# One more pair of expert-weight slots where v and the compressed rows were, and compressed columns copied unscaled in a written order of three engines

## The chip, the cores and the metric

The kernel runs on one core of one Trainium2 chip. The metric is the device time of one execution in microseconds. Everything is fp32; T = 256 tokens, D = 1024.

## What is computed

Two transformer blocks. The first is attention in two kinds, a gate, and a mixture of experts; the second a mixer, a feed-forward part and a gated projection. Cut to what matters here:

```
h = rms_norm(x, attn_norm_w)
c_q, c_kv, k_rope, dq, dk, dv, g_mla, g_diff = split(h @ w_in)        # 256, 256, 32, 5 x 1024 columns
q  = rms_norm(c_q,  mla_q_norm_w)  @ mla_w_uq                         # 16 heads x 96
kv = rms_norm(c_kv, mla_kv_norm_w) @ mla_w_ukv                        # 16 heads x (64 k + 64 v)
o_mla  = softmax attention of normed, rotated q and k
o_diff = difference of two softmax attentions with a distance bias
x = x + (sigmoid(g_mla) * o_mla + sigmoid(g_diff) * o_diff) @ w_out
h2 = rms_norm(x, ffn_norm_w)
affinity = softmax(h2 @ router_w); each of 16 experts takes its 32 best tokens
y_e = (silu(h2_e @ w_gate_e) * (h2_e @ w_up_e)) @ w_down_e            # three matrices of 8 MB per expert
x = x + the sum of the experts' rows
then a second block on x: rms_norm @ w_in, mixer, w_out, w_ff1, w_ff2, gated projection
```

## The kernel before, in words

**Stages.** The front (0 to 262 us) does the first block up to w_out. The router follows (to 277 us), then the 16 experts (to about 1165 us), then the second block. One expert's weights are 12 loads of 2 MB: four of `expert_w_gate`, four of `expert_w_up`, four of `expert_w_down`; all 192 together are some 400 MB.

**The front.** Products are made of three matmuls each (`mm3`, lines 209 to 211) of rounded parts: a weight piece is cast by ScalarE into `wh` (line 120), VectorE subtracts that from the weight into `wl` (line 121), and the pieces wait in three pairs of buffers (`split`, `put`, `take`; `AHEAD` says how many pieces are prepared ahead). `mla` begins with the transposes of x, eight `step`s over w_in's first 544 columns into four banks, the copies of these columns into `cc` (scaled by `rx`, the inverse root mean square of x: line 203 on ScalarE, line 205 on VectorE), the transposes of `cc` into the compressed rows `ch`, and then `up`: groups of six matmuls of 128x512 that go through three PSUM banks, first six groups for q (`put_q`, evicted by line 654 on ScalarE and VectorE in turn), then eight for k and v (`put_kv`, scaled by `rc`, the inverse root mean squares of the compressed rows). `rsqrt` (lines 90 to 98) is a chain of twelve small VectorE instructions. Sums of squares of q are taken by ScalarE (line 674) and reduced by VectorE (line 675). `tables` makes the tables of the rotation on GpSimd and ScalarE.

**What sets the order.** TensorE and GpSimd run in the order of the program. ScalarE and VectorE are ordered by a scheduler, except inside `manual_schedule` blocks, where they too run as written. Loads of weights are issued by SyncE's queue, in order: an issue that waits for its buffer holds up those behind it.

**The slots of the expert weights.** A ring of slots of 2 MB each is opened when the front closes. `SLOTS` names the slots of the first eleven loads: numbers from 0 are `ring2` pools (`R2` = 6 of them), -1 are two `ring1` pools, and -2 are places used once, which borrow buffers of the front (`once`: pairs of 1 MB halves loaded by line 299, or one whole). A load into a `ring2` or `ring1` slot goes through line 294, and the slot goes to the ring's end. So from load 11 on the slots come round in the order of `SLOTS` without the -2: eight slots. Load 11, the last of expert 0, takes the slot of load 0; load 12 that of load 2. In expert 0 the matmuls of the gate (line 1213) stand in turn with those that gather the tokens' rows (line 1170). The last expert closes three `ring2` slots for the second block's weight pieces; the second block's weights use the rest of the ring and `ring3` pools.

Of the kernel before, what the change touches and what calls it, by code (L numbers as in the profile page):

```python
# [23 lines left out]
R1, R2 = 4, 6  # L24
# [3 lines left out]
SLOTS = (3, -2, 2, 1, -2, 0, -1, -1, 4, 5, -2)  # L28
WSPLIT = 1088
AHEAD = 2  # L30
# [44 lines left out]
class Kernel:  # L75
# [233 lines left out]
    def run(self):  # L309
        self.cms, self.wide = {}, set()  # L310
        self.cp = self.open("cp")
        self.sm = self.open("sm", 2)
        r1 = self.ring = [self.open("ring1", side="right") for _ in range(R1)]
# [5 lines left out]
        with self.psum(mm=2, s=2, su=1, tr=2, o=1):  # L319
# [8 lines left out]
            ppool = self.open("pp", side="right")  # L328
# [16 lines left out]
            self.ring.append(self.open("ring3", side="right"))  # L345
# [5 lines left out]
            self.ring += [self.open("ring3", side="right") for _ in range(3)]  # L351
# [5 lines left out]
    def once(self):  # L357
# [7 lines left out]

        yield first
# [82 lines left out]
    def tables(self):  # L449
# [3 lines left out]
        nc.sync.dma_start(pos_c, A["positions"].rearrange("o (t p) -> p (o t)", p=128))  # L453
        pos_r = fp.tile([128, T], I32, name="pos_r")
        nc.sync.dma_start(pos_r, A["positions"].to_broadcast((128, T)))
# [20 lines left out]
        g.tensor_scalar(ang, ang, PI_IN, -PI_IN, op0=ALU.min, op1=ALU.max)  # L476
        di = fp.tile([128, NT, T], I32, name="di", tag="d1")
# [12 lines left out]
        self.lr = fp.tile([128, 4, 64], F32, name="lr")  # L490
# [11 lines left out]
    def lam(self):  # L502
# [18 lines left out]
        lp = fp.tile([128, 2, 64], F32, name="lp")  # L521
# [34 lines left out]
    def front(self):  # L556
# [19 lines left out]
        self.fp = fb = Parts(fs, (fd, same("d0", "d1")), (fv, same("v", "dist", "tab", "pos_r", "lr")),  # L576
                             (fe, same("d2")))
# [6 lines left out]
    def mla(self, fb):  # L584
        nc, A, g, ap = self.nc, self.A, self.nc.gpsimd, self.ap
        xh, xl = self.xh, self.xl
# [10 lines left out]
        with self.tc.manual_schedule(engines={mybir.EngineType.Activation, mybir.EngineType.DVE}):  # L597
            next(self.const)
            put(range(4))
            pss = [[self.bank("s"), self.bank("mm")] for t in range(NT)]  # L600
            self.ahead = 0
            self.look()
            put(range(4, 8))
            self.ahead = 1
            ws = []
            tables = self.tables()
            for k in range(8):
                ws = ws or self.take()
                step(k, *ws.pop(0))
                if k == 2:  # L610
                    next(tables)
                if k == 6:
                    next(tables)
                if k == 4:
                    self.rx = rx = self.rms(self.fa, self.x, self.od)
            cc = fb.tile([128, NT, 544], F32, name="cc", tag="d0")
# [9 lines left out]
        self.transpose_split(cc, self.col["mla_q_norm_w"], h, l, range(4), ("tr", "o", "tr", "mm"))
        sc = self.sm.tile([128, 2, NT], F32, name="sc", tag="sc")
        for i in range(2):
            self.sumsq(sc[:, i, :], cc[:, :, 256 * i : 256 * i + 256], cn[:, :, 256 * i : 256 * i + 256])
        rc = fb.tile([128, 2, NT], F32, name="rc")  # L630
        self.rsqrt(rc, sc, 1.0 / 256)

        qk = self.qp.tile([128, 2, NT, 16, 96], F32, name="qk", tag="qk")
# [566 lines left out]
    def experts(self, rp, r2, ppool, late):  # L1200
# [110 lines left out]
        for r in reversed(r2[:3]):  # L1311
            self.close(r)
# [457 lines left out]
```

## Time and profile of the kernel before

| what | us |
|---|---|
| median of three runs | 1506.15 (1505.64 to 1506.5) |
| profiled execution, its own time | 1505.89 |
| its span in the trace | 1504.2 |
| TensorE busy | 1138.1 (76%) |
| VectorE busy | 475.5 (32%) |
| ScalarE busy | 354.8 (24%) |
| DMA, mean of the span | 327 GB/s (427 in the experts) |

The page cuts the span into 40 slices of 37.6 us. TensorE is nearly always busy in slices 1 to 7 (front and router) and in the last ten (second block); in between, the DMA engines are.

### The profile page before, as it was taken

The numbers are of one execution on the slowest core, as the hardware profiler recorded it, in microseconds if no ns is written. First come the engines' busy times: TensorE is split into PE (matmuls) and PEld (weight loads), VectorE is DVE, ScalarE is ACT, GpSimd is POOL, SyncE is SP. The second block draws the span as 40 slices with busy tenths as digits, with TensorE's granted clock in tenths as the row PEclk, the third lists the DMA queues.
The fourth block names the chain that finished last, engine by engine and source line by source line (L and its number), as shares of the span: only waits on it lengthen the run. The fifth ranks groups of instructions, "written<-read, shape, count | busy, mean of one in ns | idle before, by whom it ended". The sixth has DMA issues, their size and how long they took to land.

```text
span 1504.2 us, 16611 instructions
## 1 busy us (share of the span) xinstructions
PE 1138.1 (76%) x6821; PEld 627.1 (42%) x6821; DVE 475.5 (32%) x969; ACT 354.8 (24%) x644; POOL 133.0 (9%) x181
## 2 busy tenths in 40 slices
PE   7999999885655566556565555656556899999998
PEld 6777897431111121111111111111111597889986
DVE  6987787410000000000000000000000477655456
ACT  5565655100000010000000000000000455554444
POOL 4613111000000000000000000000000134011010
PEclk9999999998688787887877888787877999999999
DMA  7533339999999999999999999999999972655520
GB/s 250 184 109 103 111 117 357 426 426 427 427 427 427 424 427 428 427 427 429 426 427 427 427 427 427 427 427 427 427 427 418 360 262 92 216 173 192 198 110 29
DMA packets 74842, 492.61 MB, mean 327 GB/s; under 512 B 5593, under 2 KB 10014, under 8 KB 50446
## 3 DMA queue, kind: packets, MB, share of 16 engines
q1 hardware_dynamic: 74366, 490.69, 80.7%
q8 instruction: 53, 0.87, 0.2%
q0 software_dynamic: 400, 0.86, 0.2%
q14 instruction: 23, 0.19, 0.0%
HBM read 490.48 MB, written 1.05 MB: 327 GB/s over the span
## 4 chain that ended last, share of the span: by engine, by line
DMA 50%; PE 37%; DVE 6%; issue 2%; ACT 1%; SPq 1%; POOL 1%; ACTq 0%; DVEq 0%
DMA w<-in_expert_w_down_dram 17%; DMA w<-in_expert_w_gate_dram 17%; DMA w<-in_expert_w_up_dram 15%; PE tr L1213 5%; PE mm L209 5%; PE mm L210 5%; PE mm L211 5%; PE acc L210 2%; PE acc L211 2%; PE acc L209 2%; DVE wl L121 2%; PE su L1261 2%; SPq L1280 1%; DMA w<-in_w_in_dram 1%; PE s L740 1%
## 5 line engine op out<-in xcount | busy, mean ns | idle before, releaser
L1213 PE MATMUL tr<-w,xe 128*32 128x512 f32 x2048 | 325.5, 768 | 207.3 <-DMA w<-in_expert_w_up_dram 121.6
L1213 PEld LDWEIGHTS tr<-w,xe 128*32 128x32 f32 x2048 | 64.7, 126 | 446.9 <-issue 162.6
L1261 PE MATMUL su<-w,hT 128*32 128x512 f32 x960 | 164.1, 821 | 92.3 <-DMA w<-in_expert_w_down_dram 84.4
L121 DVE TENSOR_TENSOR wl<-w,wh 128x1024 fp32r<-128x1024 f32 (+1 forms) x157 | 193.9, 1242 | 87.6 <-ACT wh L120 86.2
L120 ACT CAST wh<-w 128x1024 fp32r<-128x1024 f32 (+1 forms) x157 | 163.3, 1048 | 114.1 <-PE mm L211 44.9
L1239 DVE SCALAR_TENSOR_TENSOR hd<-tr,re,sg 128x512 f32<-128x512 f32 x16 | 12.0, 750 | 508.6 <-PE tr L1213 507.7
L1250 ACT ACTIVATE yh<-su,cols 128x512 fp32r<-128x512 f32 x17 | 11.7, 687 | 565.4 <-PE su L1261 528.8
L209 PE MATMUL mm<-xh,wh 128*128 128x256 f32 x448 | 128.7, 287 | 0.9 <-DVE x L1632 0.9
L210 PE MATMUL mm<-xh,wl 128*128 128x256 f32 x448 | 125.8, 281 | 0.0
L211 PE MATMUL mm<-xl,wh 128*128 128x256 f32 x448 | 125.8, 281 | 0.0
L1261 PEld LDWEIGHTS su<-w,hT 128*32 128x32 f32 x960 | 31.4, 132 | 209.4 <-DMA w<-in_expert_w_down_dram 134.3
L1251 DVE SCALAR_TENSOR_TENSOR yl<-su,cols,yh 128x512 fp32r<-128x512 f32 x17 | 12.8, 751 | 272.5 <-ACT yh L1250 272.5
L209 PEld LDWEIGHTS mm<-xh,wh 128*128 128x128 f32 x448 | 84.4, 188 | 4.0 <-issue 2.3
L210 PEld LDWEIGHTS mm<-xh,wl 128*128 128x128 f32 x448 | 84.5, 189 | 0.3
L211 PEld LDWEIGHTS mm<-xl,wh 128*128 128x128 f32 x448 | 84.4, 188 | 0.0
L1237 ACT ACTIVATE sg<-tr,re 128x512 f32<-128x512 f32 x16 | 11.0, 687 | 269.6 <-PE tr L1213 264.3
L209 PE MATMUL mm<-wh,xh 128*128 128x512 f32 (+1 forms) x140 | 57.7, 412 | 0.7 <-ACT wh L120 0.5
L1368 POOL TENSOR_SCALAR_AFFINE_SELECT m_gt<-ones 128x128 f32<-128x128 f32 x1 | 0.3, 287 | 647.6 <-DMA w<-in_expert_w_down_dram 647.6
L210 PE MATMUL mm<-wh,xl 128*128 128x512 f32 (+1 forms) x140 | 54.1, 386 | 0.0
L211 PE MATMUL mm<-wl,xh 128*128 128x512 f32 (+1 forms) x140 | 54.0, 385 | 0.0
L209 PE MATMUL acc<-wh,fhl 128*128 128x512 f32 x128 | 50.0, 391 | 0.0
L211 PE MATMUL acc<-wl,fhl 128*128 128x512 f32 x128 | 49.9, 390 | 0.0
(455 smaller groups left out, 1514.1 us busy)
## 6 DMA issues: line engine op xcount, KB each, us to landing
w<-in_expert_w_up_dram SPq DMA_DIRECT2D x64, 2048.0 KB
w<-in_expert_w_gate_dram SPq DMA_DIRECT2D x63, 2048.0 KB
w<-in_expert_w_down_dram SPq DMA_DIRECT2D x59, 2048.0 KB
w<-in_w_ff_dram SPq DMA_DIRECT2D x32, 1024.0 KB
w<-in_w_in_dram SPq DMA_DIRECT2D x29, 1024.0 KB
w<-in_expert_w_down_dram SPq DMA_DIRECT2D x10, 1024.0 KB
w<-in_w_out_dram SPq DMA_DIRECT2D x5, 1024.0 KB
w<-in_w_ple_gate_dram SPq DMA_DIRECT2D x4, 1024.0 KB
```

The lines of the kernel that those rows point to most:

```text
L120: self.nc.scalar.copy(h, src)
L121: (self.nc.gpsimd if pool else self.nc.vector).tensor_tensor(l, src, f(h), op=ALU.subtract)
L209: mm(out, ah, bh, start=start, stop=False, **kw)
L210: mm(out, al, bh, start=False, stop=False, **kw)
L211: mm(out, ah, bl, start=False, stop=stop, **kw)
L740: nc.tensor.matmul(S[:, t, :], qT[:, t * 128 : t * 128 + 128], kT, start=True, stop=True)
L1213: nc.tensor.matmul(ps[32 * j : 32 * j + 32, :], self.xe[k // 4][:, k % 4, 32 * e : 32 * e + 32], ws[k % 2][:, 0, 512 * j : 512 * j + 512], ...
L1239: nc.vector.scalar_tensor_tensor(hd, gu[1], re, sg, op0=ALU.mult, op1=ALU.mult)
L1250: nc.scalar.activation(yh, d, AF.Identity, scale=gate)
L1251: nc.vector.scalar_tensor_tensor(yl, d, gate, f(yh), op0=ALU.mult, op1=ALU.subtract)
L1261: nc.tensor.matmul(d[r : r + 32, :], hT[:, a, j, :], ws[a // 2][:, a % 2, 512 * b : 512 * b + 512], start=j == 0 and a < 2, stop=j == 3 an ...
L1280: nc.sync.dma_start(ws[j], A["expert_w_down"][0, 15, 512 * j : 512 * j + 512, 512 * b : 512 * b + 512].rearrange("(p a) n -> p a n", a=4))
```

## The change

The slots: `R2` falls to 5. A pair of pools `early` stays open from the start; in the front they hold v and the compressed rows, and afterwards the two halves of one load used once, which becomes load 0. The ring that comes round has seven slots, and load 11 takes the slot of load 2. In the second block the pair joins the ring, and later two `ring3` pools join where there were three.

The front: w_in's first columns are split in eight pieces of 544 columns where there were four of 1088 (`WSPLIT`). `cc` is copied without a scale, so it doesn't wait for `rx`; sums of squares are scaled by `rx` afterwards. The written order now covers TensorE too, and reaches through q and the factors `rc` up to the sums of squares of k's shared columns. Two blocks of idle transposes (`busy`, 8 and 6) are added to TensorE. q is evicted by ScalarE alone, and v too. The position columns come by GpSimd's queue at the very start, the rotation's sines earlier.

```diff
-R1, R2 = 4, 6
+R1, R2 = 4, 5
-SLOTS = (3, -2, 2, 1, -2, 0, -1, -1, 4, 5, -2)
-WSPLIT = 1088
+SLOTS = (-2, -2, 2, 1, -2, 0, -1, -1, 3, 4, -2)
+WSPLIT = 1024
...
+        self.early = [self.open("early", side="right") for _ in range(2)]
+        ppool = self.open("pp", side="right")
         r1 = self.ring = [self.open("ring1", side="right") for _ in range(R1)]
...
-            self.ring.append(self.open("ring3", side="right"))
+            self.ring += self.early
...
-            self.ring += [self.open("ring3", side="right") for _ in range(3)]
+            self.ring += [self.open("ring3", side="right") for _ in range(2)]
...
+        yield lambda: [tile(pool, "w") for pool in self.early]
         yield first
...
-        nc.sync.dma_start(pos_c, A["positions"].rearrange("o (t p) -> p (o t)", p=128))
+        nc.gpsimd.dma_start(pos_c, A["positions"].rearrange("o (t p) -> p (o t)", p=128))
...
-            for h in range(2):
-                for t in range(NT):
-                    self.scaled(cc[:, t, 272 * h : 272 * h + 272], pss[t][h][:, :272], rx[:, t : t + 1], t == 0)
...
-            (nc.vector.tensor_copy if t else nc.scalar.copy)(qf[:, t, n : n + 512], ps)
+            nc.scalar.copy(qf[:, t, n : n + 512], ps)
...
-            self.scaled(v[:, t, h0 : h0 + 4, :], pv[:, :, 64:128], rc[:, 1, t : t + 1], t)
+            self.scaled(v[:, t, h0 : h0 + 4, :], pv[:, :, 64:128], rc[:, 1, t : t + 1], True)
...
+        with self.tc.manual_schedule(engines=engines):
+            next(tables)
+            next(self.const)
+            put(range(4))
+            self.busy(8, "su")
...
+            for i in range(8):
+                if i == 4:
+                    for t in range(NT):
+                        nc.scalar.activation(self.od[:, t, :], x[:, t, :], AF.Square, accum_out=ss[:, t : t + 1])
+                if i == 5:
+                    next(tables)
+                if i == 6:
+                    self.ahead = 2
+                ws = ws or self.take()
+                step(i, *ws.pop(0))
...
+            for i in range(2):
+                for t in range(NT):
+                    (nc.vector.tensor_copy if t else nc.scalar.copy)(
+                        cc[:, t, 272 * i : 272 * i + 272], pss[t][i][:, :272])
+            self.busy(6, "o")
+            self.transpose_split(cc, self.col["mla_q_norm_w"], h, l, range(4), ("tr", "o", "tr", "mm"))
...
+            self.ahead = 1
+            q_in = up(0, 1536, put_q)
+            next(q_in)
+            self.rsqrt(rx, ss, 1.0 / D)
+            for _ in q_in:
+                pass
...
+            for t in range(NT):
+                nc.vector.tensor_scalar(sc[:, :, t], sc[:, :, t], rx[:, t : t + 1], rx[:, t : t + 1], op0=ALU.mult,
+                                        op1=ALU.mult)
+            self.rsqrt(rc, sc, 1.0 / 256)
+            for t in range(NT):
+                nc.vector.tensor_scalar(rc[:, :, t], rc[:, :, t], rx[:, t : t + 1], None, op0=ALU.mult)
...
-                for r in reversed(r2[3:]):
+                for r in reversed(r2[2:]):
```

VectorE from the last instructions of `rc` to the first evictions of k and v, before (`wl<-w,wh` prepares a weight piece, `qk<-mm` evicts q, `ssq<-od` reduces q's squares, `qk<-mm,rc` and `v<-mm,rc` evict k and v):

```order
L96 TENSOR_TENSOR rs_u<-rs_y 128x4
L97 SCALAR_TENSOR_TENSOR rs_u<-rs_u,rs_a 128x4
L98 SCALAR_TENSOR_TENSOR rc<-rs_u,rs_y 128x4
L654 COPY qk<-mm 128x512
L121 TENSOR_TENSOR wl<-w,wh 128x1024 x2
L654 COPY qk<-mm 128x512
L675 TENSOR_REDUCE ssq<-od 128x16
L205 TENSOR_SCALAR qk<-mm,rc 128x4x64
L121 TENSOR_TENSOR wl<-w,wh 128x1024
L205 TENSOR_SCALAR v<-mm,rc 128x256
L675 TENSOR_REDUCE ssq<-od 128x16
L205 TENSOR_SCALAR qk<-mm,rc 128x4x64
```

VectorE in the same stretch after; ahead of it stand the third weight piece of q, the twelve instructions of `rx`, two more weight pieces and the first seven of `rc`:

```order
L97 SCALAR_TENSOR_TENSOR rs_u<-rs_u,rs_a 128x4
L98 SCALAR_TENSOR_TENSOR rs_y<-rs_u,rs_y 128x4
L699 TENSOR_REDUCE ssq<-od 128x16
L96 TENSOR_TENSOR rs_u<-rs_y 128x4
L121 TENSOR_TENSOR wl<-w,wh 128x1024
L97 SCALAR_TENSOR_TENSOR rs_u<-rs_u,rs_a 128x4
L98 SCALAR_TENSOR_TENSOR rc<-rs_u,rs_y 128x4
L683 TENSOR_SCALAR rc<-rc,rx 128x2 x2
L540 SCALAR_TENSOR_TENSOR kr,skr<-cc 128x32
L699 TENSOR_REDUCE ssq<-od 128x16
L205 TENSOR_SCALAR qk<-mm,rc 128x4x64 x2
```

The evictions of q and v have left VectorE, the end of `rc` has moved behind the first reduction (line 699) and a weight piece, and both reductions stand ahead of the first k, where one did.

SyncE's queue from the last weights of w_out on, before (line 299 is a half of 1 MB; in brackets the semaphores waited for, of earlier transfers and of engines):

```order
L104 DMA w<-in_w_out_dram 128x4x512 [waits DMAHW0_49,DVE_49]
L294 DMA w<-in_expert_w_gate_dram 128x4096 [waits PE_49,DVE_49,Activation_49,Pool_49]
L299 DMA w<-in_expert_w_gate_dram 128x2048 [waits PE_49]
L294 DMA w<-in_expert_w_gate_dram 128x4096 [waits DVE_49,Activation_49]
L294 DMA w<-in_expert_w_gate_dram 128x4096 [waits PE_49]
L294 DMA w<-in_expert_w_up_dram 128x4096 [waits DMAHW1_49,DVE_49,Activation_49]
L299 DMA w<-in_expert_w_gate_dram 128x2048 [waits DVE_49,DMAHW2_49,PE_49,Pool_49]
L294 DMA w<-in_expert_w_up_dram 128x4096 [waits DMAHW3_49]
L294 DMA w<-in_expert_w_up_dram 128x4096 [waits DMAHW4_49]
L294 DMA w<-in_expert_w_up_dram 128x4096 [waits DMAHW5_49,DVE_49]
L294 DMA w<-in_expert_w_down_dram 128x4096 [waits DMAHW6_49]
L294 DMA w<-in_expert_w_down_dram 128x4096 [waits DMAHW7_49,PE_49]
```

SyncE's queue in the same stretch after; load 0's halves are not in it, since they stand further ahead among the loads of w_in, one behind the last product of `up`, one behind those of the attention that reads v:

```order
L294 DMA w<-in_expert_w_down_dram 128x4096 [waits PE_49,Pool_49]
L104 DMA w<-in_w_out_dram 128x4x512 [waits DMAHW6_49,DMAHW1_49,DVE_49]
L294 DMA w<-in_expert_w_gate_dram 128x4096 [waits DVE_49,PE_49,Activation_49]
L299 DMA w<-in_expert_w_gate_dram 128x2048 [waits PE_49]
L294 DMA w<-in_expert_w_gate_dram 128x4096 [waits PE_49]
L294 DMA w<-in_expert_w_up_dram 128x4096 [waits DMAHW2_49,DVE_49,Activation_49]
L294 DMA w<-in_expert_w_up_dram 128x4096 [waits DMAHW3_49,PE_49]
L299 DMA w<-in_expert_w_gate_dram 128x2048 [waits DMAHW4_49,DVE_49,Pool_49]
L294 DMA w<-in_expert_w_up_dram 128x4096 [waits DMAHW5_49]
L294 DMA w<-in_expert_w_up_dram 128x4096 [waits DMAHW6_49,DVE_49]
L294 DMA w<-in_expert_w_down_dram 128x4096 [waits DMAHW7_49,DMASW0_49,PE_49]
```

The first load of `w_down` has come ahead of w_out's last piece, and two loads of `w_up` where one was stand ahead of the half that waits for VectorE. Two halves of `w_down` and load 11 follow behind either list.

## Rows read from the trace of the kernel before

**Rows 1.** The page: span, shares of the chain that ended last, weight subtractions.
```profile
span 1504.2 us, 16611 instructions
...
DMA 50%; PE 37%; DVE 6%; issue 2%; ACT 1%; SPq 1%; POOL 1%; ACTq 0%; DVEq 0%
...
L121 DVE TENSOR_TENSOR wl<-w,wh 128x1024 fp32r<-128x1024 f32 (+1 forms) x157 | 193.9, 1242 | 87.6 <-ACT wh L120 86.2
```

**Rows 2.** Windows: us, busy us per engine, TensorE's granted clock, DMA share, GB/s.
```profile
251.00:255.00 4.00, 3.95 (x15) 2.29 (x14) 2.34 (x6) 2.04 (x4) 0.00 (x0) 1.00 0.09 37
277.00:291.00 14.00, 13.47 (x77) 6.20 (x78) 3.82 (x11) 1.42 (x3) 0.00 (x0) 1.00 1.01 428
344.00:1160.00 816.00, 489.64 (x2848) 112.55 (x2848) 41.31 (x81) 22.16 (x33) 0.79 (x1) 0.79 1.01 427
```

**Rows 3.** Timeline of SyncE's queue: start us, us, line, issue.
```profile
54.47 66.19 SPq L104 DMA_DIRECT2D w<-in_w_in_dram  x9
...
223.50 0.37 SPq L104 DMA_DIRECT2D w<-in_w_out_dram  x1
...
254.38 0.33 SPq L299 DMA_DIRECT2D w<-in_expert_w_gate_dram  x1
...
282.62 0.33 SPq L294 DMA_DIRECT2D w<-in_expert_w_down_dram  x1
290.88 8.40 SPq L294 DMA_DIRECT2D w<-in_expert_w_gate_dram  x4
```

**Rows 4.** Timeline of TensorE, w_out and experts 0, 1, with idle before.
```profile
253.83 0.50 PE L209 MATMUL mm<-wh,mhl 128*128 128x512 f32 x1
...
281.50 1.06 PE L1213 MATMUL tr<-w,xe 128*32 128x512 f32 x8
...
289.75 1.07 PE L1213 MATMUL tr<-w,xe 128*32 128x512 f32 x8
...
344.36 1.93 PE L1261 MATMUL su<-w,hT 128*32 128x512 f32 x16 [0.26 <-DMA w<-in_expert_w_down_dram]
```

**Rows 5.** Windows behind the issue at 223.50 into empty queues.
```profile
225.00:225.50 0.50, 0.50 (x5) 0.45 (x4) 0.24 (x1) 0.00 (x0) 0.00 (x0) 1.00 0.32 94
225.50:226.00 0.50, 0.50 (x7) 0.50 (x6) 0.50 (x4) 0.00 (x0) 0.00 (x0) 1.00 0.98 381
```

**Rows 6.** Timeline of TensorE from w_in's first columns to k, v.
```profile
26.38 0.33 PE L153 MATMUL tr<-ident,cc 128*128 128x128 f32 x1 [0.87 <-ACT cc L203]
28.46 0.33 PE L153 MATMUL tr<-ident,cc 128*128 128x128 f32 x1 [1.75 <-DVE cc L205]
...
29.36 0.80 PE L209 MATMUL mm<-wh,ch 128*128 128x512 f32 x1
...
44.24 0.47 PE L209 MATMUL mm<-wh,ch 128*128 128x512 f32 x1 [0.37 <-DVE v L205]
...
47.91 0.50 PE L211 MATMUL mm<-wl,ch 128*128 128x512 f32 x1 [0.86 <-DVE wl L121]
...
52.45 0.39 PE L211 MATMUL mm<-wl,ch 128*128 128x512 f32 x1
```

**Rows 7.** Window of q's first matmuls, with the granted clock.
```profile
29.20:32.60 3.40, 3.40 (x10) 2.45 (x9) 3.18 (x12) 2.62 (x8) 1.83 (x10) 0.51 0.93 314
```

**Rows 8.** Timeline of VectorE: the end of rc, a reduction, the first k.
```profile
36.04 0.17 DVE L98 SCALAR_TENSOR_TENSOR rc<-rs_u,rs_y 128x4 f32<-128x4 f32 x1
...
40.42 1.75 DVE L675 TENSOR_REDUCE ssq<-od 128x16 f32<-128x1536 f32 x1
42.09 0.47 DVE L205 TENSOR_SCALAR qk<-mm,rc 128x256 f32<-128x256 f32 x1
```

**Rows 9.** Timeline of ScalarE: squares of q, a weight piece's cast.
```profile
38.90 1.49 ACT L674 ACTIVATE od<-qk 128x1536 f32<-128x1536 f32 x1
40.29 1.04 ACT L120 CAST wh<-w 128x1024 fp32r<-128x1024 f32 x1
```

**Rows 10.** Waits of TensorE, second block: us, times, longest.
```profile
PE mm L209 <- ACT wh L120: 0.5, 1, 0.5
```

More of the change, by code (lines that the diff above doesn't have):

```diff
@@ L327, in run @@
             r1 = [self.open("ring1", side="right") for _ in range(R1 // 2)]
-            ppool = self.open("pp", side="right")
             r2 = [self.open("ring2", side="right") for _ in range(R2)]
@@ L476, in tables @@
         g.tensor_scalar(ang, ang, PI_IN, -PI_IN, op0=ALU.min, op1=ALU.max)
+        yield
+        nc.scalar.activation(rope, ang, AF.Sin)
+        nc.scalar.activation(self.warm, self.warm, AF.Exp)
+        pos_r = fp.tile([128, T], I32, name="pos_r")
+        nc.sync.dma_start(pos_r, A["positions"].to_broadcast((128, T)))
         di = fp.tile([128, NT, T], I32, name="di", tag="d1")
@@ L520, in lam @@
         nc.gpsimd.tensor_copy(self.onr, self.ones[:16, :])
-        lp = fp.tile([128, 2, 64], F32, name="lp")
+        lp = self.junk.rearrange("p t d -> p (t d)")[:, :128].rearrange("p (a b) -> p a b", a=2)
         ls = fp.tile([128, 2], F32, name="ls")
@@ L575, in front @@
         same = lambda *tags: dict(zip(tags, tags))
-        self.fp = fb = Parts(fs, (fd, same("d0", "d1")), (fv, same("v", "dist", "tab", "pos_r", "lr")),
-                             (fe, same("d2")))
+        self.fp = fb = Parts(fs, (fd, same("d0", "d1")), (fv, same("dist", "tab", "pos_r")),
+                             (fe, same("d2")), (self.early[0], dict(v="w")), (self.early[1], dict(ch="w")))
         self.ap = Parts(a1, (a2, same("L")), (a3, same("P")), (a4, same("PT", "jj")))
@@ L595, in step @@
                     self.mm3(pss[t][h][:, :272], xh[:, k, ts], xl[:, k, ts], wh[:, hs], wl[:, hs], k == 0, k == 7)
[L597 to L616, printed above, removed]
-            for h in range(2):
-                for t in range(NT):
-                    self.scaled(cc[:, t, 272 * h : 272 * h + 272], pss[t][h][:, :272], rx[:, t : t + 1], t == 0)
-            for _ in tables:
-                pass
-        self.ahead = AHEAD
+        engines = {mybir.EngineType.Activation, mybir.EngineType.DVE, mybir.EngineType.PE}
+        cc = fb.tile([128, NT, 544], F32, name="cc", tag="d0")
         cn = fb.tile([128, NT, 512], F32, name="cn", tag="d1")
-        ch = fb.tile([128, 2, 4, T], F32R, name="ch", tag="d2")
+        ch = fb.tile([128, 2, 4, T], F32R, name="ch")
         h, l = ch[:, 0], ch[:, 1]
[L626 to L631, printed above, removed]
+        ss = self.sm.tile([128, NT], F32, name="ss", tag="ss")
+        self.rx = rx = self.fa.tile([128, NT], F32, name="rx", tag="rx")
         qk = self.qp.tile([128, 2, NT, 16, 96], F32, name="qk", tag="qk")
@@ L651, in up @@
                         done(n0 + n, t, pss[t])
+                    yield
         def put_q(n, t, ps):
[L654 removed]
+            nc.scalar.copy(qf[:, t, n : n + 512], ps)
         def put_kv(n, t, ps):
@@ L663, in mla @@
+        self.ahead = AHEAD
         next(self.const)
@@ L691, in mla @@
             g.tensor_tensor(q2, tm[2], tm[3], op=ALU.add)
-        up(2, 2048, put_kv)
+        for _ in up(2, 2048, put_kv):
+            pass
         next(self.const)
@@ L1310, in experts @@
         self.dump("x2", self.x)
-        for r in reversed(r2[:3]):
+        for r in reversed(r2[:2]):
             self.close(r)
```

31 lines of the change are left out of this document (20 added, 11 removed).

## The prediction

> **What bounds the kernel now.** I read the page's chain first: half of it is DMA, and that is the experts' weights [rows 1]. The windows then say which stage is bound by what: in the experts the DMA queues are full from end to end (share 1.01, 427 GB/s) while TensorE works 490 of 816 us [rows 2]. There, time is bytes: a load of 2 MB takes 2.097 MB / 427 GB/s = 4.91 us, and the only question is when the stream of loads gets going and whether it ever stops. Before the experts TensorE is the bound: in the front it hardly waits after its first 53 us, so what is won or lost up to the end of the k and v products (52.45) [rows 6] is still there at the router.
>
> Two holes stand out. The DMA queues are nearly idle from 251 to 255 us (37 GB/s) [rows 2], because a half at 254.38 holds the queue [rows 3]. And between w_in's first columns and q TensorE waits 0.87 and 1.75 us for `cc` [rows 6], after which its clock is granted at half (0.51) for 3.4 us [rows 7]: q's first matmuls take 0.80 us there.
>
> **The stream of expert weights.** The change loads one more 2 MB ahead, and moves a load of `w_up` ahead of the waiting half, which fills the hole at 251. Added up that is 4.91 us + 4 us x 0.9 = 8.5 us of transfer done earlier. But the stream can only go on while slots come free. Before, load 11 takes the slot of load 0; it is issued at 282.62, right behind the matmuls at 281.50 [rows 3, 4], while the queues are still full (277 to 291: share 1.01 [rows 2]). After, load 11 takes the slot of load 2, which the matmuls at 289.75 let go at t2 = 290.88, where load 12 was issued before [rows 3, 4]. By then loads 0 to 10 have all landed, earlier than before, and the queues stand empty: the gain becomes a hole.
>
> So I compare load 12. Before: load 21 lands at 344.3, where TensorE waits for it [rows 4]; nine loads back, 344.3 - 9 x 4.91 = 300.1, is load 12, 9.2 us behind t2. After: load 11 starts into empty queues. What that costs is read from the w_out load at 223.50, which reaches full rate at about 225.5 [rows 3, 5]: 2.0 us. Load 11 lands 2.0 + 4.91 = 6.9 us behind t2, load 12 (its slot is load 3's, free some 3 us behind t2 [rows 3]) 11.8 us behind it. The stream is **2.6 us** later, less what TensorE wins on its way to t2. (Before, load 10 landed two loads ahead of load 12, at 290.3; 8.5 us earlier is 281.8, so the hole ahead of t2 is about 9 us long.) Bounds: 1.6 if the first bytes count (94 GB/s by 225.0 [rows 5]), 3.1 if the issue is half a microsecond late. A ring of seven is enough afterwards: a slot must come free within 6 x 4.91 - 2.0 = 27 us of its landing, and TensorE uses a load as it lands.
>
> The other moved issues cost nothing as long as their cover holds. The half in the place of the compressed rows waits for the last product of `up` (52.45); behind it is the w_in load issued at 54.47 [rows 3, 6]. If kv ends later, that load is later by as much. The half in v's place waits among w_in loads that wait longer themselves. The w_out piece (223.50) now stands behind 2 MB of `w_down`, 4.91 us, but its products run around 254 [rows 3, 4].
>
> The Trainium skill (DMA: Bandwidth & Descriptors, the note "436 vs ~360") lets the HBM side bind such loads at about 358 GB/s. The row above shows 427, so the trace disagrees; at 358 a load would take an estimated 5.86 us and the 2.6 would be about 4.5.
>
> **The front, to t2.** Written as the order shows it, with the durations of before.
> - Steps over w_in's first columns end near 25.4 now. Eight narrower pieces and eight idle transposes may let the clock rise sooner; squares of x move to ScalarE between the casts. I take 24.6 (23.6 to 25.6).
> - `cc`, no longer waiting for `rx`: VectorE has two weight subtractions of 1.24 us [rows 1] ahead of its copies, which I put at 25.7; four pairs of transposes, and q starts at 26.7 (26.2 to 28.3), before 29.36 [rows 6]. That is 2.7 us won. With the idle transposes in between, I take the fast clock here.
> - Six groups of six matmuls at 0.234 us (36 matmuls, 8.4 us) end q at 35.1; three groups of kv follow without any eviction, at the earliest at 39.3, with 0.7 us more for their weight pieces at 40.0. The fourth needs a bank back, so the first eviction of k.
> - That eviction is the trouble. VectorE ends q's third piece at 30.7; `rx` (twelve instructions of 0.2 us) and two diagonals bring 33.6. The next piece's cast stands on ScalarE behind q's fourth copy, its subtraction ends at 35.4, the one after at 36.8. Seven instructions of `rc`: 38.2. The first reduction waits for ScalarE's squares (1.49 us [rows 9], behind the last copy, the distances and the shared columns), which end at 38.6; with 1.67 of its 1.75 us [rows 8] unoverlapped: 40.3. A cast (1.04 us [rows 9]) and a piece: 41.8. The end of `rc` and `kr`: 42.5, where it is 36.2 before [rows 8]. Second reduction: 44.2. First k: 44.6, before 42.09 [rows 8].
> - So the fourth kv group starts at about 44.7, before 44.24 [rows 6]: all 2.7 us are gone into a wait of 4.7 us. Five groups of 1.40 us and one wait of about 1.2 for a piece (before 0.86 at 47.91) make 8.2 us: 52.9. A share of slow clock behind the wait, 0.2, makes it 53.1, against 52.7 (the last matmul at 52.45 and its end [rows 6]): **0.4 us lost**. Bounds: 0.4 won (clock fast from the beginning) to 2.9 lost (the starts at their late ends, and half a stretch of slow clock or more).
>
> VectorE is freed of three copies of q and four evictions of v behind this, ScalarE takes them beside its casts; TensorE hardly waits for either there, so zero, from 1 us won to 1 us lost (the 0.86 at 47.91 [rows 6] is the nearest row).
>
> **The last expert and the second block.** One ring slot fewer for the last `w_down` against one more during the mixer. The second block waits 0.5 us in all for a cast of weights [rows 10], which an earlier load could take away: **0.5 us won** at most by this row, none at least; I take it whole, since the pair stands open earlier than the pool it replaces. The tail I take as even, with 0.5 us lost as the bound.
>
> **Sum.** 1505.89 (the profiled execution) + 2.6 + 0.4 - 0.5 = 1508.4; that execution is 0.26 us under the median of the three runs, so 1508.6 against 1506.15. The measurement of this kernel can tell 0.2%, 3.0 us, from no change: 1503.1 and 1509.2 are the edges. The forecast's own range is 1506.5 to 1510.
>
> **Rivals.**
> - *The front's gain survives.* If the scheduler's estimate is right and VectorE reaches the first k by about 39.5, TensorE keeps the 2.7 us, loses no stretch at half clock (half of 3.4 us = 1.7) and none of 0.37 and 0.86 us [rows 6, 7]: 5.6 us. 1506.15 + 2.6 - 5.6 - 0.5 = 1502.6, faster. It decides from a front gain of 5.1 us on. For it: VectorE has less to do in this phase. Against: the order puts both reductions and two pieces ahead of the first k.
> - *The clock falls in the new wait.* TensorE stands 4 to 5 us between the third and the fourth kv group; behind waits of 0.87 and 1.75 us it was granted 0.51 for 3.4 us [rows 6, 7], which costs 1.7 us. With the late starts, the front loses 2.9: 1506.15 + 2.6 + 2.9 - 0.5 = 1511.2, slower. It decides from 0.9 us lost on. Against: kv's later groups wait for pieces anyway, which hides part of it. The Trainium skill (TensorE: Matmul & The Clock Gate, Part 1) calls the slow clock the idle state that activity releases; the stretch at 29.2 agrees (0.51 [rows 7]).
> - *The prefetch is kept.* If slots are no limit, because load 11 finds one early or expert 0 needs its loads sooner than I think, the 8.5 us count: 1506.15 - 8.5 + 0.4 - 0.5 = 1497.6. Against: every slot of the ring before load 2's is used once.
> - *Seven slots starve the stream.* One bubble of 1 us per expert would add 15 us, 1523. Against: the 27 us worked out above.
>
> **How the numbers follow.** Forecast 0.42, front's gain 0.20, clock 0.27, prefetch kept 0.08, starved 0.03. The forecast's cases lie within 0.2% but for 0.07 over it; of the front's gain I put 0.05 within. Faster: 0.15 + 0.08 = 0.23. Same: 0.35 + 0.05 = 0.40. Slower: 0.07 + 0.27 + 0.03 = 0.37. The range runs from 1501.0, which leaves out the kept prefetch and the best of the front's gain, to 1512.0, which leaves out starving and the worst of the clock.
>
> **What would show it.** In the trace after: load 11 issued within a microsecond of the end of load 2's matmuls, empty DMA queues for 9 us or more ahead of that, no hole at 251; load 12 (by the first waits for loads in experts 1 and 2) 11 to 12 us behind t2; q starting near 26.7; a wait of 4 to 5 us ahead of the fourth kv group, released by VectorE's k or ScalarE's v; kv ending near 53. I am wrong if kv ends before 50, if load 11 is issued before 288, or if the experts' windows show a DMA share under 1.

## The result, and the profile after

| | us, median | runs | ratio to before, 95% |
|---|---|---|---|
| before | 1506.33 | 1505.64 to 1508.79 | |
| after | 1518.54 | 1517.46 to 1519.53 | 1.0077 [1.0062, 1.0092] |

The change makes the kernel 12.2 us slower. The forecast was 1508.6 (1501 to 1512); the sign was left open and the size was outside the range. The profiled execution of after took 1519.5 us, 13.6 more than that of before (1505.9).

One table of TensorE and of SyncE's issues carries most of what follows. "kv end" is the start of the last matmul of the k and v products plus 0.24 us; the x8 transposes of `qk` come behind the norms of q and k; t2 is where the matmuls that read load 2 are done, which the rows of SyncE mark. Each column is one execution. Among the profiled executions of this front that differ in nothing up to there q starts between 25.73 and 27.33, so times of different executions are compared to about 1 us, and stretches within one execution better.

| place, us | before | forecast | after | later than before |
|---|---|---|---|---|
| q starts | 29.36 | 26.7 | 26.21 | -3.15 |
| fourth kv group starts | 44.24 | 44.7 | 47.55 | +3.31 |
| kv end | 52.69 | 53.1 | 57.29 | +4.60 |
| x8 transposes of `qk` | 76.46 | as before | 83.93 | +7.47 |
| t2 | 290.88 | 291.3 | 298.51 | +7.63 |
| load 21 lands | 344.36 | 347.4 | 356.70 | +12.34 |

So there are three losses up to load 21: some 4.6 us up to the end of kv, 2.9 in the norms, 4.7 in the hole of the weight stream. TensorE's timeline of after (start us, us, line, operation, and in brackets the idle time before and what ended it), which answers to [rows 6] and to the last row of [rows 4]:

```profile
26.21 0.50 PE L209 MATMUL mm<-wh,ch 128*128 128x512 f32 x1
...
39.66 0.40 PE L211 MATMUL mm<-wl,ch 128*128 128x512 f32 x1
47.55 0.80 PE L209 MATMUL mm<-wh,ch 128*128 128x512 f32 x1 [7.50 <-ACT v L203]
48.15 0.63 PE L210 MATMUL mm<-wh,ch 128*128 128x512 f32 x1
...
75.90 0.72 PE L752 MATMUL tr<-ident,qk 128*96 128x128 f32 x5 [1.94 <-DVE qk L742]
...
356.70 1.55 PE L1286 MATMUL su<-w,hT 128*32 128x512 f32 x8 [2.23 <-DMA w<-in_expert_w_down_dram]
```

q starts early and at full clock, as planned. Then TensorE stands 7.50 us where 4.7 were forecast, and goes on at half clock (0.63 us a matmul instead of 0.39). At 75.90 it waits again, 1.94 us; at the same place before it was 1.00:

```profile
69.98 0.72 PE L727 MATMUL tr<-ident,qk 128*96 128x128 f32 x5 [1.00 <-DVE qk L717]
```

SyncE's queue of after, which answers to the last two rows of [rows 3]:

```profile
298.51 0.33 SPq L294 DMA_DIRECT2D w<-in_expert_w_down_dram  x1
301.43 3.76 SPq L294 DMA_DIRECT2D w<-in_expert_w_gate_dram  x2
```

The windows of after (columns as in [rows 2]; the seventh and eighth figure are granted clock and DMA share):

```profile
47.00:54.00 7.00, 6.45 (x16) 5.12 (x17) 5.00 (x9) 4.30 (x8) 3.60 (x5) 0.55 0.32 69
76.00:86.00 10.00, 10.00 (x45) 8.32 (x45) 6.15 (x14) 4.92 (x14) 0.00 (x0) 0.83 0.33 107
...
251.00:255.00 4.00, 4.00 (x14) 1.98 (x13) 3.09 (x7) 0.41 (x1) 0.00 (x0) 1.00 1.01 430
...
284.00:288.00 4.00, 3.33 (x17) 1.82 (x17) 2.47 (x8) 0.47 (x1) 0.00 (x0) 1.00 0.44 182
288.00:292.00 4.00, 4.00 (x28) 1.72 (x24) 0.48 (x1) 0.47 (x1) 0.00 (x0) 1.00 0.00 0
292.00:296.00 4.00, 4.00 (x28) 1.72 (x24) 0.48 (x1) 0.47 (x1) 0.00 (x0) 1.00 0.00 0
296.00:300.00 4.00, 4.00 (x28) 1.72 (x24) 0.48 (x1) 0.45 (x1) 0.00 (x0) 1.00 0.35 57
...
357.00:1172.00 815.00, 496.17 (x2844) 116.62 (x2840) 41.33 (x81) 22.16 (x33) 0.82 (x1) 0.78 1.01 427
```

The hole at 251 is filled (share 1.01 where [rows 2] has 0.09). In its place the queues stand empty for some 11 us ahead of 298.51. After that the stream is as full as before: the ring of seven slots doesn't starve it.

Why the fourth kv group waits so long is on VectorE and GpSimd. VectorE of after, which answers to [rows 8] (lines 90 to 98 are the steps of `rc`'s inverse square root, line 699 is the reduction, 205 the first k):

```profile
36.63 0.16 DVE L90 TENSOR_SCALAR rs_a<-sc 128x4 f32<-128x4 f32 x1
...
37.23 0.63 DVE L96 TENSOR_TENSOR rs_u<-rs_y 128x4 f32<-128x4 f32 x1
37.89 0.66 DVE L97 SCALAR_TENSOR_TENSOR rs_u<-rs_u,rs_a 128x4 f32<-128x4 f32 x1
...
40.66 0.65 DVE L98 SCALAR_TENSOR_TENSOR rs_y<-rs_u,rs_y 128x4 f32<-128x4 f32 x1
41.23 1.74 DVE L699 TENSOR_REDUCE ssq<-od 128x16 f32<-128x1536 f32 x1
...
44.28 0.16 DVE L98 SCALAR_TENSOR_TENSOR rc<-rs_u,rs_y 128x4 f32<-128x4 f32 x1
...
46.52 0.87 DVE L205 TENSOR_SCALAR qk<-mm,rc 128x256 f32<-128x256 f32 x2
...
70.10 1.23 DVE L121 TENSOR_TENSOR wl<-w,wh 128x1024 fp32r<-128x1024 f32 x1
```

GpSimd of after in the same stretch (the rotation of q's first half):

```profile
37.09 2.83 POOL L713 TENSOR_TENSOR tm<-qk,tab 128x256 f32<-128x256 f32 x4
39.88 0.72 POOL L714 TENSOR_TENSOR qk<-tm 128x256 f32<-128x256 f32 x1
40.56 0.72 POOL L715 TENSOR_TENSOR qk<-tm 128x256 f32<-128x256 f32 x1
```

Six steps of 128x4 elements took 0.63 to 0.66 us each, as long as one GpSimd instruction (0.71), while six GpSimd instructions ran beside them. Before, the same steps took 0.17 [rows 8], with GpSimd idle.

### The profile page after: what moved, and what is told of

The parts are those of the page before. It is cut to its first block, busy times and chain, and to the rows that moved or that the text cites. A ratio compares the mean times of both kernels' runs of the same rounds, so it can differ in the third digit from the quotient of the medians.

```text
span 1517.8 us, 16661 instructions
## 1 busy us (share of the span) xinstructions
PE 1150.8 (76%) x6835; PEld 634.3 (42%) x6835; DVE 474.9 (31%) x968; ACT 359.1 (24%) x657; POOL 126.3 (8%) x184
## 4 chain that ended last, share of the span: by engine, by line
DMA 49%; PE 40%; DVE 6%; ACT 2%; issue 1%; SPq 0%; POOL 0%; ACTq 0%; DVEq 0%
DMA w<-in_expert_w_down_dram 20%; DMA w<-in_expert_w_up_dram 19%; DMA w<-in_expert_w_gate_dram 8%; PE tr L1238 5%; PE mm L209 5%; PE mm L210 5%; PE mm L211 5%; PE acc L211 2%; PE acc L210 2%; PE acc L209 2%; PE su L1286 2%; DVE wl L121 2%; PE s L765 1%; DMA w<-in_w_in_dram 1%; PE mm L1294 1%
```

## The experiments

The two traces gave a theory of separate losses: the hole of the stream, which the slots alone make, and the front's waits with their clock, which the new order of the front alone makes. Its rivals make one cause of it: the front alone, which the stream merely follows, or the slots alone. The first two runs set these apart, the others take each loss to pieces.

**The slots alone: `slots_only`.** The front of before, the slots of after.

```diff
-R1, R2 = 4, 6
+R1, R2 = 4, 5
...
-SLOTS = (3, -2, 2, 1, -2, 0, -1, -1, 4, 5, -2)
+SLOTS = (-2, -2, 2, 1, -2, 0, -1, -1, 3, 4, -2)
...
+        self.early = [self.open("early", side="right") for _ in range(2)]
```

> The slots of the changed kernel on the front of before (its order, its cc scaled by rx; the one addition needed for space: lr and lp lie in a buffer of the later attention output). Theory A (two separate losses, the stream's hole and the front): expert 0's matmuls come at the times of before (load 2 done near 290.9), load 11 is issued there, the DMA queues are empty for 8 to 13 us ahead of it, and the stream is 4 to 5 us later than before: 1510.5 to 1512. Theory B (the hole costs nothing, all of the 12 us come from the front): within 1 us of before, 1505.5 to 1507.

Measured: 1512.48 us, ratio 1.0038 [1.0024, 1.0052], +6.0 us. Its SyncE queue and TensorE:

```profile
292.29 0.33 SPq L294 DMA_DIRECT2D w<-in_expert_w_down_dram  x1
```

```profile
350.31 1.71 PE L1263 MATMUL su<-w,hT 128*32 128x512 f32 x8 [2.23 <-DMA w<-in_expert_w_down_dram]
```

t2 is 1.4 us later than before, load 21 5.95: the hole costs 4.5, as in after (12.34 - 7.63 = 4.7). It is the slots' own. The time is 0.5 us over the range of theory A, and the profiled execution (1514.57) is 2.1 over this median. The 1.4 us ahead of t2 were not expected: 0.5 are there at the end of TensorE's first wait for `cc` (26.84 for 26.38), 0.6 come in the wait ahead of the fourth kv group (1.03 us for 0.37), the rest in the router. Why is open.

**The front alone: `front_only`.** The front of after; the slots of before, that is, the lines above the other way round.

> The front of the changed kernel with the slots of before (ring of eight, no early pair). Theory A: the wait of 7.5 us ahead of the fourth kv group stays, load 2 is done near 298.5, no hole in the stream, and the whole is 7 to 8 us over before: 1513.5 to 1514.5. Theory B (front alone makes the 12 us): 1518. A third reading, that the DMA queues absorb a later front because the loads run ahead: 1507 to 1510.

Measured: 1513.05 us, ratio 1.0045 [1.0028, 1.0062], +6.6 us. TensorE waits as in after, with the ring of before:

```profile
47.10 0.80 PE L209 MATMUL mm<-wh,ch 128*128 128x512 f32 x1 [7.50 <-ACT v L203]
```

t2 (the issue of load 12) is at 296.72, +5.8 us, 1.8 ahead of the 298.5 expected: this execution starts q 0.5 us earlier than after's, and the stretch at half clock behind the same wait is 1.2 us cheaper (8.5 us instead of 9.7 from the fourth kv group to kv's end). The two halves add up to 12.6 us, the whole is 12.2: two separate losses, neither of which changes the other by more than the measurement can tell.

**The hole, filled from its end: `load0_ring`.** After, but load 0 takes a ring slot, so that load 11 can have it back early; load 2 takes the early pair.

```diff
-SLOTS = (-2, -2, 2, 1, -2, 0, -1, -1, 3, 4, -2)
+SLOTS = (2, -2, -2, 1, -2, 0, -1, -1, 3, 4, -2)
```

> The changed kernel with only the order of the first three slots changed: load 0 takes a slot of the ring, load 2 the early pair, so load 11 reuses load 0's slot. Theory A: load 11 is issued near 290.2 instead of 298.5, but load 12 then waits for load 3's slot at about 301.4 as before this edit, so a second hole opens behind load 11; the stream gains about 2 us: 1516 to 1517. Theory C (the hole is a matter of load 11 alone): 4.7 us gained, 1513.8. Theory B: nothing, 1518.5.

Measured: 1517.96 us, ratio 1.0073 [1.0056, 1.0090], 0.6 less than after, where more was expected. Its SyncE queue and windows:

```profile
290.46 0.33 SPq L294 DMA_DIRECT2D w<-in_expert_w_down_dram  x1
301.64 0.33 SPq L294 DMA_DIRECT2D w<-in_expert_w_gate_dram  x1
```

```profile
296.00:300.00 4.00, 4.00 (x28) 1.72 (x24) 0.48 (x1) 0.35 (x2) 0.00 (x0) 1.00 0.31 127
300.00:304.00 4.00, 4.00 (x44) 1.19 (x40) 0.00 (x0) 0.87 (x2) 0.00 (x0) 1.00 0.43 86
```

Load 11 goes out 8 us earlier, but load 12 then waits for the next slot, until 301.64: one hole becomes two shorter ones. Load 21 lands at 354.56, 2.1 us earlier than in after, as theory A had it; 0.8 of that is lost again in the last expert, and the time follows by 0.6 only, which these runs can't tell from nothing. So which load has which slot is worth 2 us of the hole at most; the rest is the number of slots that come free in expert 0.

**GpSimd's share of the front: `no_qrope`.** After without the rotation of q on GpSimd (that part of the computation is left out).

```diff
-            for i, qi in enumerate((q1, q2, q1, q2)):
-                g.tensor_tensor(tm[i], qi, tb[i], op=ALU.mult)
-            g.tensor_tensor(q1, tm[0], tm[1], op=ALU.subtract)
-            g.tensor_tensor(q2, tm[2], tm[3], op=ALU.add)
```

> The changed kernel without GpSimd's rotation of q (six GpSimd instructions per token half, so q is left unrotated). In the changed kernel six steps of rc's chain took 0.63 to 0.66 us each instead of 0.16 to 0.20, while GpSimd ran these instructions (37.1 to 41.2). If GpSimd's work slows VectorE's: the steps take 0.2 again, rc and the first k come 2.5 to 3 us earlier, the wait ahead of the fourth kv group falls from 7.5 to about 4.7, the time falls by 2.5 to 4 us (1514.5 to 1516). If the steps are slow for another reason: the steps stay at 0.65, 1518 to 1519.

Measured: 1515.74 us, ratio 1.0060 [1.0043, 1.0077], 2.8 less than after. Its VectorE and TensorE:

```profile
37.24 0.16 DVE L96 TENSOR_TENSOR rs_u<-rs_y 128x4 f32<-128x4 f32 x1
...
38.30 1.75 DVE L699 TENSOR_REDUCE ssq<-od 128x16 f32<-128x1536 f32 x1
...
43.60 0.86 DVE L205 TENSOR_SCALAR qk<-mm,rc 128x256 f32<-128x256 f32 x2
```

```profile
44.64 0.80 PE L209 MATMUL mm<-wh,ch 128*128 128x512 f32 x1 [4.56 <-ACT v L203]
```

The rows of VectorE up to 37.24 are those of after; the steps are back at 0.16 us, and the wait is 4.56 us, ending at 44.64. The forecast was 4.7, ending at 44.7. So what the wait has over the forecast comes from GpSimd's work beside `rc`.

**The clock in the wait: `keep_clock`.** After, with 60 idle transposes in the wait.

```diff
+                        if c0 and n0 + n == 512 and t == 0:
+                            self.busy(60, "o")
```

> The changed kernel with 60 idle transposes put behind the third kv group, to fill most of the wait of 7.5 us (60 x 0.11 = 6.6 us at the fast clock). If the stretch at half clock behind the wait (47.6 to 53.2 in the changed kernel) is a cost of its own: that stretch is granted in full, kv ends 2 to 2.8 us earlier, and 1.5 to 3 us of it reach the end: 1515.5 to 1517. If VectorE's chain to the norm of q and k sets the pace behind kv anyway: kv ends earlier but the wait there grows by as much, 1518 to 1519.

Measured: 1517.38 us, ratio 1.0070 [1.0052, 1.0088], 1.2 less than after. Its TensorE and window:

```profile
47.27 0.50 PE L209 MATMUL mm<-wh,ch 128*128 128x512 f32 x1 [0.96 <-ACT v L203]
```

```profile
47.00:54.00 7.00, 6.21 (x25) 4.62 (x26) 4.65 (x9) 4.73 (x10) 3.35 (x5) 1.00 0.39 95
```

The clock stays full (1.00 where after has 0.55), and kv ends at 55.25 instead of 57.29. Of these 2.0 us, 0.3 are an earlier start of the group and 1.7 the clock. That is the most that the clock takes here: from the fourth group to kv's end after needs 9.74 us, this run 7.98, and the four other profiled executions with the same wait (`front_only`, `load0_ring`, `no_dummies`, `norm_first`) 8.4 to 9.3. The time lies between the two expectations. The wait of 1.94 us in the norms, and the lower clock behind it (0.86 over 10 us), stayed.

**Everything behind kv: `late_both`.** The rotation of q and its squares and reductions are written behind the k and v products.

```diff
-        for t in range(NT):
-            j = self.junk.rearrange("p t d -> p (t d)")[:, :1536].rearrange("p (h d) -> p h d", d=96)
-            nc.scalar.activation(j, q[:, t], AF.Square)
-            nc.vector.tensor_reduce(sq[:, t, :], j, axis=AX.X, op=ALU.add)
+        for _ in up(2, 2048, put_kv):
+            pass
...
```

> The changed kernel with the squares and reductions of q and GpSimd's rotation of q written behind the k and v products instead of ahead of them (nothing left out). One of the two reductions then stands ahead of the first k on VectorE, and GpSimd is idle during rc's chain. If these two are what holds the first k: rc's steps take 0.2 us, the wait ahead of the fourth kv group falls from 7.5 to about 3, the time to 1513.5 to 1515. If the work is only moved (the norm of q and k waits for it later): 1517 to 1519.

Measured: 1523.81 us, ratio 1.0107 [1.0089, 1.0125], 5.3 more than after: a miss. As built, the squares are taken of the rotated q, so that the reductions wait for GpSimd as well; the wait was still 7.13 us, others of 1.86 and 1.25 came behind it, and kv ended at 62.08. GpSimd's rotation was not moved in time either: it starts at 36.75, and five steps of `rc` take 0.63 to 0.68 us as in after. The order in which the lines are written isn't the order in time. So the run doesn't do what it was made for, and it tells nothing against the reductions as a part of the wait.

**The idle transposes of the change: `no_dummies`.** After without its 8 + 6 transposes that only keep TensorE busy.

```diff
-            self.busy(8, "su")
...
-            self.busy(6, "o")
```

> The changed kernel without the two blocks of idle transposes (8 and 6). In the changed kernel the clock is full from TensorE's first transposes of x at 9.6 us, before it is half until 15.5. If the 8 idle transposes do that: without them w_in's steps run at half clock to about 15, they end some 1.5 us later, and with them everything up to the wait: 1519 to 1520. If the clock rises anyway or the wait swallows it: 1518 to 1519.

Measured: 1519.33 us, ratio 1.0084 [1.0066, 1.0102], 0.8 more than after, which these runs can't tell from nothing. Its matmuls over w_in's first columns:

```profile
13.01 0.43 PE L209 MATMUL mm<-wh,xh 128*128 128x272 f32 x1
```

They start 0.23 us apart until 13.2, as before until 15.3; in after they start 0.125 us apart from 10.7 on. That is the ratio which the larger matmuls of after show behind and ahead of the wait of 7.50 us (0.43 and 0.23 us apart), the one between TensorE's two levels, 1.2 and 2.4 GHz. The clock figure of the windows is 1.00 there in all three, so it doesn't register this stretch, and the rows decide. Of the ten profiled executions with the idle transposes eight have the short distance from 10 to 11 us on, and two (`norm_first`, `best5`) only from 14; of the three without them none has it before 13.2. That speaks for the transposes, though they don't bring the full clock forward every time. In `no_dummies` q starts at 26.86, which lies within the 25.73 to 27.33 of the executions with them: what they are worth isn't shown.

**The norms: `norm_first`.** After, with the scale of q (`rq`) computed behind k's norms.

```diff
-        self.rsqrt(rq, sq, 1.0 / 96)
...
         self.fill(2)
...
             self.fill(3)
...
+        self.rsqrt(rq, sq, 1.0 / 96)
...
```

> The changed kernel with q's inverse norms (rq) written behind the norms of k, so that on VectorE rq's end and one weight piece no longer stand ahead of the second norm of k. In all variants of the changed front the transposes of q and k are through 26.6 us behind the end of kv, in both variants of the front of before 23.8 us; TensorE waits 1.94 us for VectorE's norm there instead of 1.00 and then has half clock for about 3.4 us. If that wait is what makes the 2.9 us: the wait goes, the clock stays, 2.5 to 4 us earlier: 1514.5 to 1516. If the 2.9 us come from elsewhere: 1518 to 1519.

Measured: 1514.38 us, ratio 1.0050 [1.0035, 1.0066], 4.2 less than after. Its TensorE and window:

```profile
74.13 0.75 PE L752 MATMUL tr<-ident,qk 128*96 128x128 f32 x5 [0.65 <-POOL qk L732]
```

```profile
76.00:86.00 10.00, 10.00 (x51) 8.40 (x49) 9.01 (x24) 6.44 (x14) 1.41 (x1) 1.00 0.35 107
```

With a wait of 0.65 instead of 1.94 us the clock doesn't fall (1.00 where after has 0.83), and the stretch from kv's end to the x8 transposes takes 23.4 us instead of 26.6. The rest of the gain isn't the norms': between the two profiled executions, which are 4.6 us apart, t2 is 3.1 us earlier and the end of the last expert 1.5 us shorter. The edit takes more than one weight piece away from between the norms: two scalings of `rq` that took 2.02 us there, beside GpSimd, take 0.37 at their new place.

**Building on it.** Three kernels with the slots of before and the front of after, mended. `best2` computes `rx` between the steps over w_in and `rc` behind q's third weight piece; `best4` takes the squares of x two steps earlier and `rx` one; `best5` also has the scale of q behind k's norms.

```diff
 # best2 against front_only
                 step(i, *ws.pop(0))
+                if i == 5:
+                    self.rsqrt(rx, ss, 1.0 / D)
...
             next(q_in)
-            self.rsqrt(rx, ss, 1.0 / D)
...
+            self.rsqrt(rc, sc, 1.0 / 256)
...
             for _ in q_in:
                 pass
...
 # best4 against best2
-                if i == 4:
+                if i == 2:
...
-                if i == 5:
+                if i == 4:
```

> The slots of before with the changed front, mended: rx is made among w_in's steps, rc right behind the third weight piece of q, so both stand ahead of the kv weight pieces, and nothing but these pieces is ahead of the first k. Theory: no long wait ahead of the fourth kv group, q starts near 26.2, kv ends near 48 to 49.5 (52.7 before), no hole in the stream; 2 to 4.5 us of the gain reach load 2 and the end: 1502 to 1504.5, faster than before. Rival (VectorE is full to 70 us, so the norm of q and k comes as before): 1505.5 to 1506.5.

Measured: 1510.19 us, ratio 1.0009 [0.9998, 1.0020]: no gain where one was expected. Its ten runs lie in two groups, four at 1506.2 to 1506.5 and six at 1510.2 to 1511.3, the profiled one in the upper; why is open. In the profile the long wait is gone, but twelve small instructions of `rx` now stand ahead of the copies of `cc`, and TensorE waits 2.62 us for these and goes on at half clock.

> The mended front with the slots of before, squares of x two steps earlier on ScalarE and rx one step earlier on VectorE, so that rx fills VectorE's idle time among w_in's steps and no longer stands ahead of the last pieces (it cost a wait of 2.6 us and the clock in the version before). q should start near 25.5 to 26.5 at full clock and kv end near 48 to 50; with the 2.9 us lost at the norm of k the end is 1 to 3 us before the kernel before: ratio 0.998 to 0.9993. If kv ends at 52 or later: ratio 1.001 to 1.003.

Measured: 1505.24 us, ratio 0.9994 [0.9985, 1.0004], which can't be told from before. q starts at 25.73, kv ends at 48.62, 4.1 us ahead of before; t2 is at 288.17, 2.7 ahead. The wait of 1.94 us for the norms is still there, but here the clock doesn't fall behind it:

```profile
67.24 0.72 PE L750 MATMUL tr<-ident,qk 128*96 128x128 f32 x5 [1.94 <-DVE qk L740]
```

```profile
66.00:72.00 6.00, 4.76 (x24) 4.09 (x25) 4.59 (x6) 1.78 (x3) 0.00 (x0) 1.00 0.44 119
72.00:78.00 6.00, 6.00 (x32) 5.02 (x31) 5.12 (x14) 4.87 (x13) 0.34 (x1) 1.00 0.16 58
```

The stretch from kv's end to the x8 transposes takes 25.1 us, 1.5 less than in after and 1.3 more than before: the same wait without its half clock. In the eight other profiled executions with this wait the clock fell.

> As the mended front above (best4), with rq behind the norms of k as well. If both gains add up, load 2 is done 5 to 7 us earlier than in the kernel before and the stream of experts with it: ratio 0.9955 to 0.9975. If the stream doesn't follow the front (its loads are bound by their slots or by w_out's loads): ratio 0.998 to 1.000.

Measured: 1503.72 us, ratio 0.9982 [0.9973, 0.9991], 14.8 us less than after and 0.2% faster than before, less than was expected. Its SyncE queue, windows and TensorE, and at last the row of before that answers to TensorE's (load 22 lands):

```profile
280.59 0.33 SPq L294 DMA_DIRECT2D w<-in_expert_w_down_dram  x1
288.85 3.25 SPq L294 DMA_DIRECT2D w<-in_expert_w_gate_dram  x2
```

```profile
280.00:284.00 4.00, 4.00 (x28) 1.72 (x24) 0.35 (x2) 0.47 (x1) 0.00 (x0) 1.00 0.89 289
284.00:288.00 4.00, 4.00 (x28) 1.72 (x24) 0.35 (x2) 0.47 (x1) 0.00 (x0) 1.00 0.83 352
288.00:292.00 4.00, 4.00 (x36) 1.42 (x32) 0.31 (x1) 0.47 (x1) 0.00 (x0) 1.00 0.61 160
```

```profile
346.76 1.92 PE L1284 MATMUL su<-w,hT 128*32 128x512 f32 x16 [2.36 <-DMA w<-in_expert_w_down_dram]
```

```profile
349.26 2.85 PE L1261 MATMUL su<-w,hT 128*32 128x512 f32 x16 [2.97 <-DMA w<-in_expert_w_down_dram]
```

t2 is 2.0 us earlier than before instead of 5 to 7, and load 22 is 2.5 earlier. Of the missing gain 1.5 us are this execution's start: q starts at 27.25, in `best4` with the same order up to there at 25.73. And the queues are no longer full from 280 on (289, 352 and, at load 12, 160 GB/s, where [rows 2] has 428): with loads that come earlier the ring of eight slots begins to open a hole in the same place.

## Why the prediction was wrong, step by step

**The weight stream: right mechanism, wrong size.** Load 11 went out behind load 2's matmuls into queues that had long been empty, the hole at 251 was filled, and seven slots were enough, all as forecast. The term was 2.6 us (1.6 to 3.1) and measured 4.5 to 4.7. The step that failed is the place of load 12 before, 300.1, got by going nine loads back from the landing of load 21. The bytes tell it better:

```profile
0.00:290.88 290.88, 271.21 (x1582) 217.08 (x1583) 222.14 (x558) 156.32 (x357) 79.90 (x122) 0.98 0.57 200
```

```profile
0.00:298.51 298.51, 274.25 (x1596) 218.98 (x1597) 221.46 (x557) 160.60 (x370) 73.22 (x125) 0.97 0.54 191
```

These windows, of before and then of after, end at t2. Before, 290.88 us x 200 GB/s = 58.2 MB had come by then; after, 298.51 x 191 = 57.0 MB. The rates are rounded, so the difference of 1.2 MB is good to 0.3; `slots_only` has 57.0 too (292.29 us at 195 GB/s). At t2 before had 1.2 MB of load 11 already, so that load 12 was complete, by bytes, 0.9 + 2.1 = 3.0 MB or 7.1 us behind t2, not 9.2. After it was 2 x 4.91 us and a start behind it: with the 2.0 us that the forecast took for the start, 11.8 - 7.1 = 4.7. The window from t2 of after to the landing of load 21 tells the rest:

```profile
298.51:356.70 58.19, 47.78 (x347) 17.25 (x347) 10.48 (x20) 6.33 (x9) 0.00 (x0) 0.97 0.99 413
```

58.19 us x 413 GB/s = 24.0 MB, which take 56.3 us at 427 GB/s: the start cost 1.9 us (1.6 in `slots_only`), so it was sized right. Loads 11 to 21 are 23.1 MB, so about 1 MB of later loads was in when load 21 landed. That is the 2 us by which going back from a landing put load 12 of before too late. All of it is worked out from the windows and was not tried by itself.

The Trainium skill (DMA: Bandwidth & Descriptors, the note "436 vs ~360") led the prediction to an estimate of about 4.5. That it meets the measured size is luck: behind the hole the share is 1.01 at 427 GB/s.

**The front up to q: right.** 26.21 for 26.7, at full clock. The forecast allowed that the idle transposes let the clock rise sooner; the matmul rows of `no_dummies` speak for that, but its q starts within the range of the executions with them, so what it is worth isn't shown.

**The fourth kv group: the step `rc` failed.** "Seven instructions of `rc`: 38.2" took each at its price of before, 0.17 us and a gap. The chain began on time (36.63 for 36.8), but six of its steps took 4.1 us where 1.2 were allowed, and the first reduction began at 41.23 instead of 38.6, because GpSimd's rotation of q, which needs q alone and not `rc`, now ran beside them; `no_qrope` shows it. From there the delay went on to the first k and the fourth group. It was to be seen ahead: in the trace of before GpSimd pays for the meeting. VectorE, then GpSimd, before:

```profile
42.48 1.22 DVE L121 TENSOR_TENSOR wl<-w,wh 128x1024 fp32r<-128x1024 f32 x1
```

```profile
42.50 1.78 POOL L690 TENSOR_TENSOR qk<-tm 128x256 f32<-128x256 f32 x1
```

A GpSimd instruction of 0.7 us (0.72 in the same place after) took 1.78 beside a VectorE subtraction of 1.22. The Trainium skill (SBUF — State Buffer, "Who interferes with whom") says that a VectorE instruction with two inputs in SBUF and a GpSimd instruction that reads SBUF exclude each other, and that `tensor_reduce` never contends. Both traces agree: the one that starts later waits for the other (0.16 becomes 0.66, 0.7 becomes 1.78), and the reductions kept their 1.74 us.

**The clock behind the wait: named, too small.** The forecast gave it 0.2 us, and its rival ended at 1511.2 with 2.9 us lost in the front. Against the forecast's own steps, the fourth group starts 2.85 us late, and the groups from there on take 9.74 us instead of 8.4: 57.29 for 53.1. The wait of 7.50 us was followed by 7 us at a mean clock of 0.55. The 9.74 is the largest of five executions with this wait (8.4 to 9.7), so of the 1.3 us over the forecast some is this execution's.

**Behind kv: the step "zero" failed.** The forecast put 1 us at most on it, from a wait of 0.86. VectorE does one more weight subtraction (1.23 us at 70.10) ahead of k's norms than before. It makes the wait 1.94 instead of 1.00 us, plus 0.19 beside it, and behind that the clock falls: 10 us at 0.83 hold 3.4 us of half clock, 1.7 us lost. Together 2.8 of the 2.9 measured. `best4`, with the same wait and no fall of the clock, keeps 1.3 of them, and `norm_first`, without the wait, takes 3.2 back; that the one subtraction makes the wait is read from the rows and wasn't tried by itself. The forecast followed VectorE's order only to the first evictions of k, and thought of the evictions of q and v alone.

**The last expert and the second block: the 0.5 us was not won.** From the first transposes of the second block to the end both kernels take 324.8 us. Ahead of them, from the last wait for a load of `w_up` in expert 15, it took 15.9 us before and 17.3 after, and between 15.7 and 18.1 in the others, also with the slots of before (17.4 in `front_only`). The mean clock in this stretch goes with it: 1.00 before, 0.70 after, 0.67 where it took 18.1. The forecast has no term for that; it isn't shown to come from the change.

From the forecast to the measurement: 2.5 forecast, and missed 2.1 in the hole, 4.2 up to the end of kv, 2.9 in the norms and the 0.5 not won make 12.2, the difference of the medians. That it comes out so exactly is luck, since the terms are those of two profiled executions, which are 13.6 us apart with the 1.4 of the last expert.

## What to carry to other kernels

A prefetch pays only as far as the slots behind it: ask when the next slot comes free, count the bytes that had already moved by that time in the kernel before, and price the hole by them. Where a change moves small VectorE steps, look at what GpSimd does beside them at the new place; a chain of six cost 3 us more here. A new idle stretch ahead of TensorE costs its length and, in most executions here, a stretch of half clock behind it, and an engine made free may be filled with work that stands ahead of what TensorE waits for.

## What was not expected of the hardware

- VectorE's 128x4 steps with two inputs took 0.63 to 0.66 us beside GpSimd instructions of 0.71, and 0.16 without them; the reductions beside GpSimd did not change. It isn't only steps of two tensors: the scalings of q's sums (TENSOR_SCALAR, 128x16) took 0.70 and 0.58 us beside the second half's rotation in after, 0.29 and 0.28 in `no_qrope`.
- Behind a wait of 1.94 us the clock fell in eight of nine profiled executions (0.83 to 0.86 over 10 us) and stayed full in one (`best4`); behind waits of 1.00 (before) and 0.65 (`norm_first`) at the same place it did not fall. So the length of the wait alone doesn't settle it.
- Behind one and the same wait of 7.50 us the kv groups took 8.4 to 9.7 us in five executions, 8.0 with the wait filled.
- A stop of 11 us in the stream of 2 MB loads cost 4.5 to 4.7 us: 1.6 to 1.9 for the start, and the rest for the 1.2 MB that before had moved of load 11 by then.
